# Order of the projections in two attention mixers: queries and keys first, values next, the gate last

## The chip, the cores and the metric

One core of a Trainium2 chip runs the whole program in one launch. The metric is the device time in microseconds, from the first to the last instruction of one execution and what lies around them; several executions are timed and the median counts. Engines are named as in the profile: PE (TensorE matmul), PEld (its weight loads), DVE (VectorE), ACT (ScalarE), POOL (GpSimd), SP (SyncE, whose queue issues the DMAs). Each engine works off its own queue in order; semaphores hold an instruction until its inputs are there.

## The reference

Two layers over 256 tokens of width 1024, all in float32. Each layer is a mixer and then a PEER expert lookup; each of these begins with an RMS norm whose scale and shift come from a conditioning vector (adaLN), and ends in a gated residual.

```python
# layer 0, mixer: h (256 x 1024) -> y
z = h @ w_in                                   # mq mk mv mo mi mf bq bk bv
qk = silu(causal_depthwise_conv(concat(mq, mk), conv_w))
hm = mlstm_chunkwise(q, k, mv, mi + igate_b, mf + fgate_b)     # 4 heads of 128, chunks of 128 tokens
hm = rms_norm(hm, mnorm_g) * sigmoid(mo)       # output gate
qb, kb = rms_norm(bq, qn_g), rms_norm(bk, kn_g)                # 8 heads of 64
hb = softmax(qb kb^T * scale - slope * dist, causal) @ bv      # one block of 256: plain causal attention
y = concat(hm, hb) @ w_out

# layer 1, mixer: differential attention, 8 heads, two q/k parts of 64, values of 128
q, k, v = split(h @ w_in);  q, k = rms_norm(q), rms_norm(k)
o = (softmax(q1 k1^T ...) - lam * softmax(q2 k2^T ...)) @ v
y = (rms_norm(o, onorm_g) * (1 - lam_init)) @ w_out

# both layers, PEER: 8 heads, product keys 2 x 128, top 16, 16384 experts
x = x + g2 * sum(gate * gelu(u[idx] . h2) * v[idx])
```

## The kernel before

**Matmuls.** A float32 product is made of three passes. A weight tile of 128 x 1024 is loaded (`raw`), ACT rounds it to a high part (`hi`, line 155), DVE subtracts that from it (`lo`, line 158), and PE takes high by high, high by low and low by high. There are three buffers each of `hi` and `lo`. A column tile (`mm_col`, lines 181 to 183) gives 128 output columns on the partitions for 256 tokens: 24 matmuls of 256 columns. A row weight (`mm_row`, lines 233 to 235) gives a quarter of the sum for 512 output columns with the tokens on the partitions: 12 matmuls of 512 columns; four row weights make one row product, in two PSUM buffers.

**Order.** The kernel is written as generators. A mixer's main generator yields after each column tile or row weight (a step); at each step `advance` moves every running side generator (`live`: head pairs, the mLSTM, the norm of q and k) on by one piece. From a certain step on (`SIDE_AT`, `SIDE1_AT`) a step also issues one adaLN product: a 512 KB load and one DVE operation of line 248. `take` keeps weights loaded and split two or three steps ahead in the order of `self.feed`. The framework's planner then sets each engine's order by its own estimate of when inputs are ready, with what is traced earlier going first. `tc.issue_after(x)` adds an edge to it: what is traced under it on the engine of `x` is queued behind `x`, without waiting for `x` to end.

**Mixer 0** (`mixer0`). Column tiles: i = 0 the gate inputs of the mLSTM, 1 to 8 its q and k with the convolution (three DVE operations each, line 509), 9 to 12 its output gate `mo`. Row products of four weights each: the mLSTM's values `mv`, the attention's values `bv`, then q and k of heads 0 to 3 and of heads 4 to 7. `ROWS0` says how many row weights follow each column tile: one each after tiles 4 to 7, twelve after tile 8. The mLSTM starts after all 16. A row product of q and k goes to `qk_norm`: squares on ACT, sums on DVE, the power -1/2 on POOL (`qr`, line 258), the product by it on DVE (`zn`, line 374), transposes on PE (line 382), copies to `z` on ACT. Each head pair then runs `moba_pair`: logits (line 398, in the two PSUM buffers `l`), softmax (lines 408 to 412 and 550), transposes (419 to 421), output (563 to 566). At the end of the mLSTM comes `my`, its output by the gate (line 712). The output projection (`residual`) takes the rows of heads 0 to 5 first, then the mLSTM's, then those of the last two heads.

**Mixer 1** (`mixer1`). Row products in the order q and k of heads 0-1, of 2-3, values of heads 0 to 3, q and k of 4-5, of 6-7, values of 4 to 7. `diff_head` runs logits and two softmaxes per head (784, 785 combine them), waits until its values are there, then transposes, output, norm (`on`, line 808, with the power `oss` on POOL) and the high and low parts for the output projection (814, 815). Softmax tiles `sm_p` have 12 buffers in both mixers.

PSUM has eight buffers: tags `h` and `g` two each, and in the mixers `l` and `t` two each.

Of the kernel before, what the change touches and what calls it, by code (L numbers as in the profile page):

```python
# [20 lines left out]
P = 128  # L21
# [21 lines left out]
LATEP = (None, None, (None, 3))  # L43
ROWS0 = {4: 1, 5: 1, 6: 1, 7: 1, 8: 12}
AHEAD = 2
# [29 lines left out]
class Prog:  # L75
# [251 lines left out]
    def alibi(self, pool):  # L327

        nc = self.nc
        di = pool.tile([P, T], I32, tag="sm_p", name="dist_i", bufs=12)  # L330
# [24 lines left out]
    def qk_norm(self, pool, pss, heads):  # L355
# [16 lines left out]
        for ps, r in zip(pss, rs):  # L372
            z = pool.tile([P, 512], F32, tag="zn", name="zn", bufs=QK_ROWS)
            nc.vector.tensor_tensor(out=split(z), in0=split(ps), in1=r.unsqueeze(2).to_broadcast([P, 8, 64]), op=ALU.mult)
            zn.append(z)
        yield
        for i, begin in enumerate(heads):
# [24 lines left out]
    def softmax(self, pool, lg, h, qt, bias):  # L402

        nc = self.nc
        n = P * (qt + 1)
        p = pool.tile([P, T], F32, tag="sm_p", name="sm_p", bufs=12)
        st = pool.tile([P, 4], F32, tag="sm_s", name="sm_s", bufs=24)
# [17 lines left out]

    def residual(self, layer, gate, w_out, act, kds):
        nc = self.nc
        for dt, ps in self.col_tiles([w_out[i] for i in range(KD)], act, ("h", "h", "l"), kds):
# [13 lines left out]
    def mixer0(self):  # L442
        nc, tc = self.nc, self.tc
        with ExitStack() as st:
# [36 lines left out]
            cols = [w_in[c] for c in cols]  # L481
            row_aps = [self.io["ev_v"][n, w4] for n in range(2) for w4 in range(4)]
            row_aps += [self.io["ev_qk"][n, w4] for n in range(2) for w4 in range(4)]
            self.feed, n = [], 0
            for i in range(3, 13):
                self.feed.append(cols[i])
                self.feed += row_aps[n:n + ROWS0.get(i, 0)]
                n += ROWS0.get(i, 0)
            row_steps = [self.project_rows(lambda w4, n=n: self.io["ev_v"][n, w4], h, dst)
                         for n, dst in ((0, mv[:, :, :, :P]), (1, bv))]  # L490

            def pairs(n):
                heads = [lambda zs, hp=2 * n + k: live.append(self.moba_pair(pool, hp, zs, bv[:, :, 0], bias, yhi, ylo))
                         for k in range(2)]
                return self.qk_rows(pool, lambda w4: self.io["ev_qk"][n, w4], h, "gh"[n],
                                    lambda pss: live.append(self.qk_norm(pool, pss, heads)))
            row_steps = chain(*row_steps, pairs(0), pairs(1))
            nrow, started = 0, False
            tag0 = lambda i: "t" if min(ROWS0) < i <= max(ROWS0) else "h" if i < 9 or i > 10 else "g"
            for i, ps in self.col_tiles(cols, h, ("h", "h", "l"), ws=ws, rest=tag0):  # L500
                if i == 0:
# [9 lines left out]
                else:  # L511
                    nc.scalar.copy(mo[:, i - 9, :], ps)
                if i == 6:
                    bias = self.alibi(pool)
# [12 lines left out]
                for _ in range(ROWS0.get(i, 0)):  # L527
                    next(row_steps)
                    nrow += 1
                    self.advance(live)  # L530
                    yield
                if i >= 8 and nrow >= 4 and not started:
                    live.append(self.mlstm(pool, rows, qk, mv, mo, yhi, ylo))
                    started = True
            while live:
                self.advance(live)
            yield from self.residual(0, 16, self.io["ev_out"], (yhi, ylo), (4, 5, 6, 0, 1, 2, 3, 7))

    def moba_pair(self, pool, hp, zs, bv, bias, yhi, ylo):

# [6 lines left out]
        for qt in range(TT):  # L547
            for hh in range(2):
                p, rc, n = self.softmax(pool, lgs[hh], 2 * hp + hh, qt, bias)
                nc.vector.tensor_scalar_mul(p[:, :n], p[:, :n], rc)  # L550
                pr[hh].append(p)
            yield
        pts = []
# [166 lines left out]
    def mixer1(self):  # L720
# [4 lines left out]
        with ExitStack() as st:  # L725
# [7 lines left out]
            with tc.issue_after(self.last_h.ins), tc.issue_after(self.last_t.ins):  # L733
                self.qk_setup(pool, Cols.od_qn, Cols.od_kn)
                og = pool.tile([P, 1], F32, name="og")
                nc.vector.tensor_scalar_mul(og, self.small[:, Cols.onorm:Cols.onorm + 1], 1.0 - LAM_INIT)
                bias = self.alibi(pool)
            v = pool.tile([P, TT, 1024], F32, name="v")
# [16 lines left out]
            self.ready = ws  # L755
            self.feed = od_qk[0][3:] + od_qk[1] + od_v[0] + od_qk[2] + od_qk[3] + od_v[1]
            for i, _ in enumerate(chain(heads(0, "h"), heads(1, "g"), values(0), heads(2, "g"), heads(3, "h"), values(1))):
                if i == 5:
# [11 lines left out]
            while live:  # L770
                self.advance(live)
            yield from self.residual(1, 16, self.io["od_out"], (yhi, ylo), range(KD))

# [472 lines left out]
```

## Time and profile before

| | us |
|---|---|
| median of 3 runs | 1953.21 (1952.89 to 1954.54) |
| the profiled execution | 1958.02 |
| its span, first to last instruction | 1956.2 |
| mean granted PE clock | 0.987 |

The span holds, in this order: loading and the first norm (to 33 us), mixer 0 (to 190), PEER of layer 0 (to 1000), mixer 1 (to 1143) and PEER of layer 1. The granted clock is a share of PE's full 2.4 GHz. A row of a view that ends in `[3.43 <-DVE sm_s L408]` says that the engine was idle for 3.43 us before the instruction and what ended that.

### The profile page before, as it was taken

The page shows a single profiled execution, that of the slowest core. Times are in us where ns is not written, and L with a number is a line of the kernel's source. Part 1 is how long each engine was busy: PE and PEld are TensorE (multiplying, and loading weights), DVE is VectorE, ACT ScalarE, POOL GpSimd, SP SyncE. Part 2 cuts the span into 40 slices and gives each one's busy share as a digit, 9 for nine tenths or more (in the row PEclk, how much of TensorE's full clock was granted, in tenths as well). Part 3 has the DMA queues.
Part 4 walks back from the last instruction along what each step waited for, and adds up shares of the span by engine and source line. Part 5 has one row for each costly group of instructions (what it writes and reads, how often), then busy time and mean ns, then how long its engine had stood idle before and what let it go on. Part 6 is the DMA issues. An engine that isn't in the chain of part 4 may idle for free.

```text
span 1956.2 us, 31712 instructions
## 1 busy us (share of the span) xinstructions
PE 1895.7 (97%) x11733; PEld 1666.4 (85%) x11733; DVE 1524.4 (78%) x3183; ACT 1164.1 (60%) x2249; POOL 40.5 (2%) x37
## 2 busy tenths in 40 slices
PE   4988999999999999999999999999999999999999
PEld 4877999989999788888877799999999988888887
DVE  8886999789998656688568889988899965556655
ACT  4664555688876544444446654568888754444443
POOL 0010000000000000000001200000000000000000
PEclk9999999999999999999989999999999999999999
DMA  8872355555555677898447343554555556669760
GB/s 326 291 255 66 122 171 189 170 164 162 170 159 177 196 216 222 301 366 294 147 150 248 119 146 117 184 183 157 168 164 167 165 172 194 194 199 358 226 197 22
DMA packets 103979, 376.24 MB, mean 192 GB/s; under 512 B 11536, under 2 KB 12944, under 8 KB 103696
## 3 DMA queue, kind: packets, MB, share of 16 engines
q1 hardware_dynamic: 103824, 374.22, 57.7%
q8 instruction: 92, 1.51, 0.3%
q14 instruction: 63, 0.52, 0.1%
HBM read 373.12 MB, written 1.05 MB: 191 GB/s over the span
## 4 chain that ended last, share of the span: by engine, by line
PE 84%; DVE 7%; issue 4%; ACT 2%; DMA 1%; POOL 1%; POOLq 0%; DVEq 0%; ACTq 0%
PE ps_h L976 13%; PE ps_acc L928 12%; PE ps_acc L929 12%; PE ps_acc L927 12%; PE ps_h L181 7%; PE ps_h L183 7%; PE ps_h L182 7%; PE ps_h L980 6%; PE ps_g L1131 3%; DVE lo L158 2%; DVE raw L248 2%; PE ps_acc L999 1%; DMA raw<-in_ev_qk_dram 1%; POOL qr L258 1%; ACT hi L155 1%
## 5 line engine op out<-in xcount | busy, mean ns | idle before, releaser
L155 ACT CAST hi<-raw 128x1024 fp32r<-128x1024 f32 x613 | 645.5, 1054 | 585.2 <-PE ps_acc L928 309.8
L158 DVE TENSOR_TENSOR lo<-raw,hi 128x1024 fp32r<-128x1024 f32 x613 | 747.9, 1221 | 303.1 <-ACT hi L155 296.0
L927 PE MATMUL ps_acc<-hi,act 128*128 128x512 f32 x1024 | 398.2, 390 | 4.4 <-ACT act L908 4.4
L928 PE MATMUL ps_acc<-hi,act 128*128 128x512 f32 x1024 | 400.5, 391 | 0.3 <-DVE act L909 0.2
L929 PE MATMUL ps_acc<-lo,act 128*128 128x512 f32 x1024 | 400.5, 391 | 0.0
L976 PE MATMUL ps_h<-h,hi 128*128 128x512 f32 x1088 | 391.1, 400 | 0.0
L181 PE MATMUL ps_h<-h,hi 128*128 128x256 f32 x1216 | 349.9, 288 | 6.9 <-ACT h L465 3.4
L183 PE MATMUL ps_h<-h,lo 128*128 128x256 f32 x1216 | 345.9, 285 | 0.5 <-DVE lo L158 0.4
L182 PE MATMUL ps_h<-h,hi 128*128 128x256 f32 x1216 | 345.4, 284 | 0.8 <-DVE h L467 0.8
L980 PE MATMUL ps_h<-h,lo 128*128 128x256 f32 x1088 | 281.4, 279 | 0.0
L181 PEld LDWEIGHTS ps_h<-h,hi 128*128 128x128 f32 x1216 | 233.9, 193 | 9.2 <-ACT h L465 4.5
L182 PEld LDWEIGHTS ps_h<-h,hi 128*128 128x128 f32 x1216 | 234.1, 193 | 3.5 <-DVE h L467 1.3
L183 PEld LDWEIGHTS ps_h<-h,lo 128*128 128x128 f32 x1216 | 233.9, 192 | 1.9 <-DVE lo L158 1.2
L976 PEld LDWEIGHTS ps_h<-h,hi 128*128 128x128 f32 x1088 | 201.0, 188 | 35.3
L927 PEld LDWEIGHTS ps_acc<-hi,act 128*128 128x128 f32 x1024 | 192.4, 188 | 44.8 <-ACT act L908 4.8
L928 PEld LDWEIGHTS ps_acc<-hi,act 128*128 128x128 f32 x1024 | 193.1, 189 | 41.2 <-DVE act L909 1.2
L929 PEld LDWEIGHTS ps_acc<-lo,act 128*128 128x128 f32 x1024 | 193.2, 189 | 40.5 <-DVE lo L158 0.7
L980 PEld LDWEIGHTS ps_h<-h,lo 128*128 128x128 f32 x1088 | 205.0, 188 | 8.5 <-DVE lo L158 0.5
L248 DVE CUSTOM_DVE_ANT_0 raw<-raw,crow,small 128x1024 f32<-128x1024 f32 x96 | 122.5, 1279 | 22.0 <-DMA raw<-in_ada_w_dram 21.9
L1108 ACT ACTIVATE oi<-iota,it 128x128 f16<-128x128 f16 x320 | 107.9, 402 | 0.0
L1118 DVE TENSOR_TENSOR og<-oj,gt 128x1024 f16<-128x1024 f16 x128 | 87.6, 684 | 3.5 <-PE ps_g L1131 2.8
L984 ACT COPY hs<-ps_h 128x256 f32<-128x256 f32 x136 | 51.1, 376 | 58.0 <-PE ps_h L976 57.8
(318 smaller groups left out, 2240.8 us busy)
## 6 DMA issues: line engine op xcount, KB each, us to landing
raw<-in_uT_dram SPq DMA_DIRECT2D x256, 512.0 KB, 3.6
raw<-in_v_dram SPq DMA_DIRECT2D x256, 512.0 KB, 4.4
raw<-in_ada_w_dram SPq DMA_DIRECT2D x96, 512.0 KB, 5.2
raw<-in_wq_dram SPq DMA_DIRECT2D x32, 512.0 KB, 4.8
raw<-in_od_qk_dram SPq DMA_DIRECT2D x16, 512.0 KB, 5.2
raw<-in_ev_in_dram SPq DMA_DIRECT2D x13, 512.0 KB, 5.4
raw<-in_ev_v_dram SPq DMA_DIRECT2D x8, 512.0 KB, 4.5
raw<-in_ev_qk_dram SPq DMA_DIRECT2D x8, 512.0 KB, 5.2
```

Of the source, the lines that this page charges most:

```text
L155: nc.scalar.copy(hi, raw)
L158: self.last_lo = nc.vector.tensor_tensor(out=lo, in0=raw, in1=hi.bitcast(F32), op=ALU.subtract)
L181: nc.tensor.matmul(ps, lhsT=whi[:, s], rhs=ahi[:, kd, :], start=kd == kds[0], stop=False)
L182: nc.tensor.matmul(ps, lhsT=whi[:, s], rhs=alo[:, kd, :], start=False, stop=False)
L183: nc.tensor.matmul(ps, lhsT=wlo[:, s], rhs=ahi[:, kd, :], start=False, stop=kd == kds[-1])
L248: nc.vector.tensor_tensor_reduce(w, w, self.crow, 1.0, self.small[:, ab:ab + 1], ALU.mult, ALU.add, m)
L927: nc.tensor.matmul(acc[q], lhsT=xhi, rhs=vhi[:, c], start=m == 0, stop=False)
L928: nc.tensor.matmul(acc[q], lhsT=xlo, rhs=vhi[:, c], start=False, stop=False)
L929: nc.tensor.matmul(acc[q], lhsT=xhi, rhs=vlo[:, c], start=False, stop=m == NEXP - 1)
L976: wide = lambda: nc.tensor.matmul(ps, lhsT=whi[:, s], rhs=both[:, kd].rearrange("p a t -> p (a t)"), start=kd == 0, stop=kd == KD - 1)
L980: nc.tensor.matmul(ps[:, :T], lhsT=wlo[:, s], rhs=both[:, kd, 0], start=False, stop=False)
L1108: nc.scalar.activation(oi[:, k, :], self.iota, AF.Square, scale=-1.0, bias=tabs["i"][:, t0 + k:t0 + k + 1])
```

## The change

Mixer 0 now projects q and k of heads 0 to 3 after column tile 4 and, after tile 8, `mv`, q and k of heads 4 to 7, and `bv`. The mLSTM starts when 8 row weights are through (before: 16). A head pair waits with its transposes until `bv` is projected. The mask of the attention is set up at tile 3 instead of 6. The output projection takes all heads' rows first and the mLSTM's last. Column tiles past the third and the row products change PSUM tags. Mixer 1 projects q and k of all heads, then all values, and has 20 buffers of `sm_p`. In both, each `zn` product is queued behind the low part that was traced last, and the two products of a pair come one step apart.

```diff
-ROWS0 = {4: 1, 5: 1, 6: 1, 7: 1, 8: 12}
+ROWS0 = {4: 4, 8: 12}
...
             z = pool.tile([P, 512], F32, tag="zn", name="zn", bufs=QK_ROWS)
-            nc.vector.tensor_tensor(out=split(z), in0=split(ps), in1=r.unsqueeze(2).to_broadcast([P, 8, 64]), op=ALU.mult)
+            with self.tc.issue_after(self.last_lo.ins):
+                nc.vector.tensor_tensor(out=split(z), in0=split(ps), in1=r.unsqueeze(2).to_broadcast([P, 8, 64]),
+                                        op=ALU.mult)
             zn.append(z)
-        yield
+            yield
...
-        p = pool.tile([P, T], F32, tag="sm_p", name="sm_p", bufs=12)
+        p = pool.tile([P, T], F32, tag="sm_p", name="sm_p", bufs=self.n_p)
...
-            row_aps = [self.io["ev_v"][n, w4] for n in range(2) for w4 in range(4)]
-            row_aps += [self.io["ev_qk"][n, w4] for n in range(2) for w4 in range(4)]
+            row_aps = [self.io[name][n, w4] for n in range(2) for name in ("ev_qk", "ev_v") for w4 in range(4)]
...
-            row_steps = chain(*row_steps, pairs(0), pairs(1))
-            nrow, started = 0, False
-            tag0 = lambda i: "t" if min(ROWS0) < i <= max(ROWS0) else "h" if i < 9 or i > 10 else "g"
-            for i, ps in self.col_tiles(cols, h, ("h", "h", "l"), ws=ws, rest=tag0):
+            row_steps = chain(pairs(0), row_steps[0], pairs(1), row_steps[1])
+            nrow = 0
+            for i, ps in self.col_tiles(cols, h, ("h", "h", "l"), ws=ws):
...
+                    if nrow == 16:
+                        rows["bv"] = True
                     self.advance(live)
                     yield
-                if i >= 8 and nrow >= 4 and not started:
-                    live.append(self.mlstm(pool, rows, qk, mv, mo, yhi, ylo))
-                    started = True
+                    if nrow == 8:
+                        live.append(self.mlstm(pool, rows, qk, mv, mo, yhi, ylo))
...
-            yield from self.residual(0, 16, self.io["ev_out"], (yhi, ylo), (4, 5, 6, 0, 1, 2, 3, 7))
+            yield from self.residual(0, 16, self.io["ev_out"], (yhi, ylo), (4, 5, 6, 7, 0, 1, 2, 3), ("g", "g", "l"))
...
+        while not rows.get("bv"):
+            yield
...
+                self.n_p = 20
...
-            self.feed = od_qk[0][3:] + od_qk[1] + od_v[0] + od_qk[2] + od_qk[3] + od_v[1]
-            for i, _ in enumerate(chain(heads(0, "h"), heads(1, "g"), values(0), heads(2, "g"), heads(3, "h"), values(1))):
+            self.feed = od_qk[0][3:] + od_qk[1] + od_qk[2] + od_qk[3] + od_v[0] + od_v[1]
+            for i, _ in enumerate(chain(*[heads(n, "hg"[n % 2]) for n in range(4)], values(0), values(1))):
```

## Rows read from the trace of the kernel before

**Rows 1.** The page's first part: busy us (share of the span) and instructions.
```profile
PE 1895.7 (97%) x11733; PEld 1666.4 (85%) x11733; DVE 1524.4 (78%) x3183; ACT 1164.1 (60%) x2249; POOL 40.5 (2%) x37
```

**Rows 2.** Busy time by stretch: length, PE, PEld, DVE, ACT, POOL, clock, DMA.
```profile
75.20:168.80 93.60, 81.49 (x463) 67.52 (x461) 77.02 (x207) 51.74 (x121) 10.13 (x5) 0.91 0.62 214
1006.60:1122.30 115.70, 107.15 (x538) 85.51 (x538) 98.79 (x303) 73.70 (x190) 23.45 (x17) 0.94 0.51 173
...
75.20:110.30 35.10, 34.08 (x154) 27.63 (x153) 30.14 (x45) 17.16 (x22) 4.15 (x2) 1.00 0.88 308
```

**Rows 3.** The same view, short stretches of row weights, output tiles, and behind a stall.
```profile
98.00:105.00 7.00, 7.00 (x32) 5.79 (x32) 5.56 (x10) 3.65 (x4) 3.28 (x2) 1.00 1.03 367
174.00:186.00 12.00, 12.00 (x102) 12.00 (x102) 9.82 (x15) 6.37 (x10) 0.00 (x0) 1.00 0.02 3
1046.00:1050.50 4.50, 4.50 (x11) 3.53 (x12) 4.27 (x22) 1.03 (x5) 0.00 (x0) 0.51 1.01 380
```

**Rows 4.** Timeline of PE, logits: start us, length us, instruction, count.
```profile
122.79 2.24 PE L398 MATMUL ps_l<-z 64*128 64x256 f32 x8 [3.43 <-DVE sm_s L408]
...
1036.14 0.92 PE L398 MATMUL ps_l<-z 64*128 64x256 f32 x8
...
1043.97 1.99 PE L398 MATMUL ps_l<-z 64*128 64x256 f32 x8 [3.71 <-DVE sm_s L408]
```

**Rows 5.** Waits of PE, 0 to 200 and 930 to 1200 us: total, times, longest.
```profile
PE ps_l L398 <- DVE sm_s L408: 3.4, 1, 3.4
...
PE ps_l L398 <- DVE sm_s L408: 4.4, 2, 3.7
```

**Rows 6.** Waits of DVE, 42.9 to 168.8 and 1006.6 to 1122.3 us.
```profile
DVE ylo L566 <- ACT yhi L565: 3.1, 3, 1.5
DVE zn L374 <- POOL qr L258: 3.0, 2, 1.5
DVE sm_s L412 <- ACT sm_p L411: 2.0, 3, 1.4
...
DVE mnum L701 <- POOL mr L258: 1.8, 1, 1.8
DVE my L712 <- PE ps_t L709: 1.4, 1, 1.4
...
DVE on L808 <- POOL oss L258: 5.1, 7, 2.2
DVE zn L374 <- POOL qr L258: 3.8, 4, 1.5
```

**Rows 7.** Timeline of DVE around the second pair's products in mixer 1.
```profile
1037.72 0.69 DVE L374 TENSOR_TENSOR zn<-ps_g,qr 128x512 f32<-128x512 f32 x1 [1.17 <-POOL qr L258]
...
1038.40 1.22 DVE L158 TENSOR_TENSOR lo<-raw,hi 128x1024 fp32r<-128x1024 f32 x1
1041.14 0.69 DVE L374 TENSOR_TENSOR zn<-ps_g,qr 128x512 f32<-128x512 f32 x1 [1.53 <-POOL qr L258]
```

**Rows 8.** Groups by line, 33 to 190 us: count, busy us, mean ns, idle before.
```profile
L158 DVE TENSOR_TENSOR lo<-raw,hi 128x1024 fp32r<-128x1024 f32 x38 | 46.2, 1217 | 3.7 <-ACT hi L155 3.3 <-ACT qsq L362 0.3
...
L248 DVE CUSTOM_DVE_ANT_0 raw<-raw,crow,small 128x1024 f32<-128x1024 f32 x28 | 35.6, 1277 | 4.0 <-DMA raw<-in_ada_w_dram 4.0
```

**Rows 9.** Timeline of ACT: the sigmoid of the output gate in mixer 0.
```profile
141.18 1.28 ACT L518 ACT_TABLE_LOAD   x1
142.47 1.06 ACT L518 ACTIVATE mo<-mo 128x1024 f32<-128x1024 f32 x1
```

**Rows 10.** Line 258, the powers (ns, min/median/max), and the timeline beside a pair.
```profile
L258 POOL TENSOR_TENSOR qr<-qv,mhalf x12: 1632/2492/2743, 101.7 to 1091.8; 128x8 f32<-128x8 f32 x12
...
1024.33 4.15 POOL L258 TENSOR_TENSOR qr<-qv,mhalf 128x8 f32<-128x8 f32 x2 [7.11 <-DVE qv L365]
...
1025.52 1.23 DVE L158 TENSOR_TENSOR lo<-raw,hi 128x1024 fp32r<-128x1024 f32 x1
```

**Rows 11.** Busy time by stretch of the instructions on `sm_p` alone: DVE.
```profile
1006.60:1122.30 115.70, 21.81 (x64) 0.94 0.51 173
```

More of the change, by code (lines that the diff above doesn't have):

```diff
@@ L329, in alibi @@
         nc = self.nc
-        di = pool.tile([P, T], I32, tag="sm_p", name="dist_i", bufs=12)
+        di = pool.tile([P, T], I32, tag="sm_p", name="dist_i", bufs=self.n_p)
         nc.gpsimd.iota(di, pattern=[[-1, T]], base=P, channel_multiplier=1)
@@ L424, in transpose_p, with residual @@
         return pt
-    def residual(self, layer, gate, w_out, act, kds):
+    def residual(self, layer, gate, w_out, act, kds, tags):
         nc = self.nc
-        for dt, ps in self.col_tiles([w_out[i] for i in range(KD)], act, ("h", "h", "l"), kds):
+        for dt, ps in self.col_tiles([w_out[i] for i in range(KD)], act, tags, kds):
             g = self.mod[:, layer, gate + dt:gate + dt + 1]
@@ L488, in mixer0 @@
                 n += ROWS0.get(i, 0)
-            row_steps = [self.project_rows(lambda w4, n=n: self.io["ev_v"][n, w4], h, dst)
+            row_steps = [self.project_rows(lambda w4, n=n: self.io["ev_v"][n, w4], h, dst, "g")
                          for n, dst in ((0, mv[:, :, :, :P]), (1, bv))]
             def pairs(n):
-                heads = [lambda zs, hp=2 * n + k: live.append(self.moba_pair(pool, hp, zs, bv[:, :, 0], bias, yhi, ylo))
+                heads = [lambda zs, hp=2 * n + k: live.append(self.moba_pair(pool, hp, zs, bv[:, :, 0], bias, yhi, ylo, rows))
                          for k in range(2)]
@@ L512, in mixer0 @@
                     nc.scalar.copy(mo[:, i - 9, :], ps)
-                if i == 6:
+                if i == 3:
+                    self.n_p = 12
                     bias = self.alibi(pool)
@@ L529, in mixer0, with moba_pair @@
                     nrow += 1
+                    if nrow == 16:
+                        rows["bv"] = True
                     self.advance(live)
                     yield
-                if i >= 8 and nrow >= 4 and not started:
-                    live.append(self.mlstm(pool, rows, qk, mv, mo, yhi, ylo))
-                    started = True
+                    if nrow == 8:
+                        live.append(self.mlstm(pool, rows, qk, mv, mo, yhi, ylo))
             while live:
                 self.advance(live)
-            yield from self.residual(0, 16, self.io["ev_out"], (yhi, ylo), (4, 5, 6, 0, 1, 2, 3, 7))
-    def moba_pair(self, pool, hp, zs, bv, bias, yhi, ylo):
+            yield from self.residual(0, 16, self.io["ev_out"], (yhi, ylo), (4, 5, 6, 7, 0, 1, 2, 3), ("g", "g", "l"))
+    def moba_pair(self, pool, hp, zs, bv, bias, yhi, ylo, rows):
         nc = self.nc
@@ L771, in mixer1 @@
                 self.advance(live)
-            yield from self.residual(1, 16, self.io["od_out"], (yhi, ylo), range(KD))
+            yield from self.residual(1, 16, self.io["od_out"], (yhi, ylo), range(KD), ("h", "h", "l"))
     def diff_head(self, pool, hd, zs, v, vhave, bias, lam, og, yhi, ylo):
```

## The prediction

> **What bounds the kernel now.** I read the page first, for who is busy over the whole span, and then only the two mixer stages, since the change touches nothing else. The reader is to see in the page's row that TensorE (PE) is busy 97% of the span [rows 1]: outside the mixers nothing is left to gain by order. So the question is how much of the mixers' time PE does not need.
>
> Second view, busy time in two stretches [rows 2]. The first goes from 75.2 us (nine column tiles and four row weights are through PE, which the new order also has done by then) to 168.8 (the last low part of the attention output is written). The second goes from 1006.6 (first operation of layer 1's norm) to 1122.3 (the same last low part). VectorE (DVE) is busy 77.0 of 93.6 us and 98.8 of 115.7 us: idle 16.6 and 16.9 us.
>
> PE's need is counted from how many matmuls it starts in a stretch without gaps (one of the count is the pieces cut at the ends): 31 of 512 columns in 7.00 us and 101 of 256 in 12.00 [rows 3], so 0.227 and 0.12 us for one, 2.73 for a row weight (12 of them) and 2.9 for a column tile (24). The first stretch holds 12 row weights, four gate tiles and about half of three output tiles: 32.8 + 11.6 + 4, and some 22 us of small matmuls, counted in the same way (for instance four times 0.92 for the logits [rows 4]): 70 of 93.6 us. The second holds 24 weights, most of three tiles (7) and some 26 of small ones: 99 of 115.7. So each stretch has 17 to 23 us that PE doesn't need, and a floor nearly as near on DVE. Neither engine alone explains the loss; the waits between them do.
>
> Third view, who waited for whom. On PE [rows 5] the largest wait inside each of the two stages is that of a logits matmul for a softmax on DVE, 3.4 us and 3.7. Each costs more than its row. Before the stall eight logits matmuls took 0.92 us, right after it 2.24 and 1.99, and from 1046.0 on only some 10 of 512 columns start in 4.50 us, at a granted clock of 0.51 [rows 3]: PE stood still and came back at 1.2 GHz instead of 2.4. The stall of 3.71 is followed by 1.1 us (logits) and some 2 (ten matmuls where 20 would fit) lost in this way: 6.8 in all; the one of mixer 0 comes to about 6 likewise (3.4 + 1.3 + some 1.4).
>
> On DVE [rows 6] I look for waits that stand in its queue with runnable work behind them. The norm-factor product `zn` waits 3.0 us in mixer 0 and 3.8 in mixer 1 for GpSimd's power; `on` waits 5.1 for the same engine; in mixer 0's end `ylo`, `sm_s`, `mnum`, `my` wait 3.1 + 2.0 + 1.8 + 1.4 = 8.3. The order of time shows what a `zn` wait holds up [rows 7]: product (1.17 late), then a weight's low part, then the second product (1.53 late), and only behind that the first softmax of layer 1, for which PE's second logits wait until 1043.97.
>
> **The change part by part.** All sums are against the profiled execution: span 1956.2, 1.8 around it, 1958.0 in all, which is 4.8 over the median of the runs, 1953.2. I take the gain off the median.
>
> *Products behind a later low part.* Each of the 12 pieces (4 + 8) of `zn` now follows the low part of a weight that is used two or three weights later, and the second one is traced a step after the first. The rows show a low part directly behind a product (1038.40 behind 1037.72), so the pin does change DVE's order. A low part takes 1.22 us and the adaLN product that often stands next to it 1.28 [rows 8], about the 1.17 to 1.53 that DVE stood still: the wait is filled, -3.0 and -3.8 of DVE time. What is queued behind `zn`: transposes on PE, z on ScalarE, logits, softmax; and the PSUM pair, which the heads after next need. Those start four weights after the product's own rows end (11 us), the product follows some two weights after, so I price this at nothing; bounds 0 to 3 us (one weight late, once).
>
> *Mixer 0, q and k of the first four heads before the values.* Nothing is added or removed: 37 weight loads, 16 of them row weights, 24 adaLN loads in between from the same step on, all on SP in the new order with the ring of 8. The logits of heads 0 to 3 move from 113 to about 78 us, under row projections; the mLSTM starts after 8 row steps instead of 16, some 22 us sooner. So in the end stretch fewer chains are left, and the 8.3 us of DVE waits there shrink. They don't vanish: the gate is last, and after its fourth tile come copy 0.4, table load 1.28, sigmoid 1.06 [rows 9], the product `my` 1.1, the high part 0.6, the low part 0.7, and 1.8 more for the second half: 7 us. Cover for it is heads' output rows first in the output projection: three tiles by four rows by three matmuls by 0.12 = 4.3 us, so 2.7 are exposed. I take half of 8.3 as gained, 4.2 (bounds 0 and 8.3), and 0.8 for the PE slow time beyond DVE's gain. Sum for mixer 0: 3.0 + 4.2 + 0.8 = 8. Bounds: 0, and DVE's 16.6.
>
> *Gate transposes of the mLSTM.* They take a third buffer of the ring that the first pair now holds, so they wait for its product; their column copy is needed first at the mLSTM's start, 20 us later. Nothing. The new PSUM names in the output projection: nothing, the buffers are drained by then.
>
> *Mixer 1, all heads before the values.* Again no operation more. The second four heads' logits come three weights (8 us) sooner, heads 0 and 1 one step later; the first four heads' outputs wait for the values, eight weights later than before. Gained: the two `zn` waits ahead of the first softmax, and with them the 6.8 us on PE. On DVE: 3.8, and of the 5.1 of `on` the piece that stood behind a `qr` on GpSimd's queue, 2.2, since all `qr` now precede all `oss`; the rest is the chain at the end and stays. About 1 more at the end, where the last two heads' softmaxes no longer follow the last row weight. Sum 7. Bounds: 0, and 16.9.
>
> *20 buffers for the softmax tiles.* Eight heads hold two each until the values are there, and those in flight some more. Eight more KB may make early loads of layer 1 wait for other old tiles; they run 25 us ahead of use. Nothing.
>
> Total: 8 + 7 = 15 off 1953.2: 1938.
>
> *A rule weighed.* The rows have GpSimd's power at 1.63 to 2.74 us for one and the same shape [rows 10]. A low part that began inside a pair of powers (1025.52, in 1024.33 to 1028.48) took 1.23, no longer than any other. The Trainium skill (SBUF — State Buffer, section "Who interferes with whom") says that a VectorE instruction with two SBUF inputs and a GpSimd one that reads SBUF exclude each other, and that the second "fully blocks". By that rule the low part put in the product's place would wait just as long. The trace shows GpSimd's time vary, and no block of DVE.
>
> **The rivals.**
> 1. *Forecast*, the waits named above go: 1938, own range 1930 to 1946; chance 0.48.
> 2. *Most of the floor is reached*: with more runnable work at every time DVE's idle of 33.5 us falls to a fifth: -27, 1926. For it: the waits are short and of many kinds, which is what a wider choice cures. Against: the chains at the start and end of both stages stay, where DVE has little else to do. 0.15.
> 3. *DVE is the bound and gives it back*: the work goes earlier into a stretch where DVE has little room (12 row weights with an adaLN product each), other waits replace those gone: -4, 1949. For it: DVE 30.1 of 35.1 us busy from 75.2 to 110.3 [rows 2]. 0.2, half of it inside the bound of no change.
> 4. *Slower: DVE overrun in mixer 1's q and k stage.* Place: 1035 to 1080. For four weights DVE must do four low parts 4.9, four adaLN products 5.1, two heads' norm 2.8 (two products of 0.69, two reduces taken as long) and softmax 2 x 2.7 (21.81 over eight heads [rows 11]) plus about 1 of small ones: 19. PE needs 10.9 + 1.8 + 1.2 = 13.9. Without value weights between, nothing lets DVE catch up, low parts come late, and PE stalls. Today one such stall costs 6.8; three of them, one for each pair after the first, make 13.6 more than today, against 8 from mixer 0: +6, 1959. Decides from about two stalls of that length. Against: adaLN products needn't come early. 0.11.
> 5. *The product's wait moves onto the low part* (the mutual exclusion): of the 15 the 6.8 of `zn` are lost, 1945. The row at 1025.52 speaks against it. 0.06.
>
> **How the numbers follow.** A measurement of this kernel can't tell 0.2%, 4 us, from no change: faster is under 1949.3, slower over 1957.1. Faster: 0.47 + 0.15 + 0.10 + 0.06 = 0.78; same 0.01 + 0.10 = 0.11; slower 0.11. The range 1923 to 1953 holds the forecast, most of rival 2, all of 3 and 5; outside are rival 4 and the far part of 2.
>
> **What would show it.** Right: `zn` with no idle of DVE before it; the logits waits of 3.4 and 3.7 gone from PE; mixer 0's last `ylo` near 161 and mixer 1's stretch some 7 us shorter; the stages of the expert mixers unchanged in length. Wrong: PE waiting for `lo` in mixer 1's row stage with the clock granted below 1.0 there (rival 4); DVE's idle in both stretches as large as now (rival 3); a low part near 2.5 us beside a power (rival 5); a stall of more than 5 us between the sigmoid and the output projection.

## The result, and the profile after

The changed kernel takes 1934.37 us (median of 3 runs, 1933.43 to 1937.32) where the kernel before took 1953.21: ratio 0.990, 95% interval 0.9886 to 0.9913. Forecast was 1938, in a range of 1923 to 1953.

The profiled execution took 1934.37 as well (span 1932.6), against 1958.02 before. To see where the 23.6 us went I cut both executions at the start of the matmuls that spread a stage's norm factors (line 302). They stand at each mixer's end and at the start of the second mixer. Rows of the kernel after, the first and last start at the end of each row:

```profile
L302 PE MATMUL ps_g<-ident,nr x4: 275/275/376, 175.7 to 176.1; 128*128 128x128 f32 x4
...
L302 PE MATMUL ps_g<-ident,nr x4: 421/421/580, 989.7 to 990.5; 128*128 128x128 f32 x4
...
L302 PE MATMUL ps_g<-ident,nr x4: 275/275/376, 1120.9 to 1121.4; 128*128 128x128 f32 x4
```

| us | up to mixer 0's end | expert stage 0 | mixer 1 | rest |
|---|---|---|---|---|
| before | 191.4 | 813.9 | 138.9 | 812.0 |
| after | 175.7 | 814.0 | 131.2 | 811.7 |
| difference | -15.7 | +0.1 | -7.7 | -0.3 |

So both mixers pay, the expert stages nothing. Forecast were 8 and 7. (The sum is 23.6 and not the medians' 18.8 because the profiled execution before stood 4.8 over its median.)

Busy time of the two stretches that answer to the first two of [rows 2] (same columns; again from nine column tiles and four row weights done, and from the second norm's first operation, to the last low part of the attention output):

```profile
76.40:152.90 76.50, 72.28 (x453) 60.25 (x453) 72.65 (x205) 51.89 (x126) 6.84 (x3) 1.00 0.76 258
990.90:1100.80 109.90, 104.25 (x523) 83.33 (x523) 98.17 (x303) 74.01 (x190) 22.88 (x17) 0.96 0.53 182
```

The first stretch is 17.1 us shorter. DVE's idle time in it fell from 16.6 us to 76.50 - 72.65 = 3.9, which is 12.7; the other 4.4 is DVE work that now lies outside the stretch, 2.4 of it two adaLN products behind it, beside the output projection. The granted clock rose from 0.91 to 1.00. In the second stretch DVE's idle fell from 16.9 to 11.7 and the clock rose from 0.94 to 0.96.

What waits are left on DVE, 44 to 152.9 us and 990.9 to 1100.8, against [rows 6]: no `zn` in either, `ylo` 3.1 became 0.4, `my` 1.4 became 0.3, and no wait for an adaLN transfer, of which there were 4.0 us [rows 8].

```profile
DVE mnum L705 <- POOL mr L258: 1.5, 1, 1.5
DVE lo L158 <- ACT hi L155: 1.4, 2, 1.0
...
DVE ylo L570 <- ACT yhi L569: 0.4, 1, 0.4
...
DVE my L716 <- PE ps_t L713: 0.3, 1, 0.3
...
DVE on L813 <- POOL oss L258: 4.5, 6, 0.9
...
DVE sm_s L414 <- ACT sm_p L413: 1.8, 4, 0.9
```

On PE, 44 to 200 and 990 to 1120 us, the waits for a softmax of 3.4 and 3.7 [rows 5] are gone; others, smaller, have come at both mixers' ends:

```profile
PE ps_t L421 <- ACT pT L425: 2.9, 2, 1.8
...
PE ps_t L818 <- DVE ylo L820: 2.7, 3, 1.4
```

And the place of [rows 7] in mixer 1's second group: DVE goes from a low part straight to the product, does softmax work and one more low part, and takes the second product, with no idle time in brackets anywhere:

```profile
1038.33 1.22 DVE L158 TENSOR_TENSOR lo<-raw,hi 128x1024 fp32r<-128x1024 f32 x1
1039.47 0.68 DVE L375 TENSOR_TENSOR zn<-ps_h,qr 128x512 f32<-128x512 f32 x1
...
1040.68 1.22 DVE L158 TENSOR_TENSOR lo<-raw,hi 128x1024 fp32r<-128x1024 f32 x1
...
1041.96 0.67 DVE L375 TENSOR_TENSOR zn<-ps_h,qr 128x512 f32<-128x512 f32 x1
```

### The profile page after: what moved, and what is told of

It is laid out like the page before. It is cut to its first block, busy times and chain, and to the rows that moved or that the text cites. A ratio compares the mean times of both kernels' runs of the same rounds, so it can differ in the third digit from the quotient of the medians.

```text
span 1932.6 us, 31700 instructions
## 1 busy us (share of the span) xinstructions
PE 1884.6 (98%) x11733; PEld 1657.8 (86%) x11733; DVE 1522.5 (79%) x3183; ACT 1161.8 (60%) x2247; POOL 40.6 (2%) x37
## 4 chain that ended last, share of the span: by engine, by line
PE 89%; issue 5%; DVE 4%; ACT 1%; DMA 1%; POOL 0%; POOLq 0%; SPq 0%; ACTq 0%; DVEq 0%
PE ps_h L981 13%; PE ps_acc L933 12%; PE ps_acc L934 12%; PE ps_acc L932 12%; PE ps_h L181 7%; PE ps_h L183 7%; PE ps_h L182 7%; PE ps_h L985 7%; PE ps_g L1136 3%; DVE lo L158 1%; PE ps_g L234 1%; PE ps_g L235 1%; PE ps_g L233 1%; PE ps_h L233 1%; PE ps_h L235 1%
## 5 line engine op out<-in xcount | busy, mean ns | idle before, releaser
L181 PE MATMUL ps_h<-h,hi 128*128 128x256 f32 x1264 | 362.9, 287 | 7.0 <-ACT h L467 3.7
L183 PE MATMUL ps_h<-h,lo 128*128 128x256 f32 x1264 | 358.9, 284 | 0.4 <-DVE lo L158 0.4
L182 PE MATMUL ps_h<-h,hi 128*128 128x256 f32 x1264 | 358.3, 283 | 0.8 <-DVE h L469 0.8
L985 PE MATMUL ps_h<-h,lo 128*128 128x256 f32 x1088 | 281.4, 279 | 0.0
L181 PEld LDWEIGHTS ps_h<-h,hi 128*128 128x128 f32 x1264 | 242.4, 192 | 9.4 <-ACT h L467 4.7
L182 PEld LDWEIGHTS ps_h<-h,hi 128*128 128x128 f32 x1264 | 242.7, 192 | 3.6 <-DVE h L469 1.3
L183 PEld LDWEIGHTS ps_h<-h,lo 128*128 128x128 f32 x1264 | 242.4, 192 | 1.8 <-DVE lo L158 1.1
L981 PEld LDWEIGHTS ps_h<-h,hi 128*128 128x128 f32 x1088 | 201.0, 188 | 35.3
L985 PEld LDWEIGHTS ps_h<-h,lo 128*128 128x128 f32 x1088 | 205.0, 188 | 8.5 <-DVE lo L158 0.5
```

The lines of the kernel that those rows point to most:

```text
L181: nc.tensor.matmul(ps, lhsT=whi[:, s], rhs=ahi[:, kd, :], start=kd == kds[0], stop=False)
L182: nc.tensor.matmul(ps, lhsT=whi[:, s], rhs=alo[:, kd, :], start=False, stop=False)
L183: nc.tensor.matmul(ps, lhsT=wlo[:, s], rhs=ahi[:, kd, :], start=False, stop=kd == kds[-1])
L981: wide = lambda: nc.tensor.matmul(ps, lhsT=whi[:, s], rhs=both[:, kd].rearrange("p a t -> p (a t)"), start=kd == 0, stop=kd == KD - 1)
L985: nc.tensor.matmul(ps[:, :T], lhsT=wlo[:, s], rhs=both[:, kd, 0], start=False, stop=False)
```

## The experiments

There were twelve runs. Their times spread by several us from execution to execution of one kernel (last section), so the four stage lengths of each profiled execution, cut as above, are read beside the whole time.

| kernel | median us | ratio to before, 95% interval | mixer 0's end | expert 0 | mixer 1 | rest |
|---|---|---|---|---|---|---|
| e1 pin only | 1945.44 | 0.9935 to 0.9964 | 186.5 | 811.3 | 134.2 | 812.2 |
| e2 order only | 1939.71 | 0.9914 to 0.9940 | 175.4 | 812.2 | 138.0 | 811.6 |
| e3 mixer 0 and pin | 1935.77 | 0.9899 to 0.9928 | 175.4 | 811.5 | 133.4 | 812.2 |
| e4 mixer 1 and pin | 1943.49 | 0.9926 to 0.9952 | 187.7 | 811.4 | 131.0 | 811.6 |
| e5 the changed kernel again | 1934.53 | 0.9878 to 0.9908 | 176.3 | 814.0 | 130.9 | 811.7 |
| e6 late mLSTM | 1937.39 | 0.9907 to 0.9934 | 181.7 | 811.4 | 129.5 | 811.6 |
| e7 old output order | 1930.76 | 0.9870 to 0.9901 | 174.3 | 811.7 | 132.3 | 810.0 |
| e8 one step | 1930.55 | 0.9865 to 0.9895 | 173.7 | 815.3 | 132.8 | 811.1 |
| e9 step apart in mixer 1 | 1931.05 | 0.9854 to 0.9887 | 173.7 | 815.0 | 131.6 | 811.6 |
| e10 gate before values | 1929.57 | 0.9852 to 0.9882 | 174.6 | 811.8 | 131.1 | 811.7 |
| e11 values between | 1932.88 | 0.9872 to 0.9911 | 172.6 | 812.2 | 136.8 | 810.1 |
| e12 early mLSTM alone | 1945.48 | 0.9931 to 0.9963 | 185.2 | 811.7 | 135.1 | 811.2 |

The kernel before ran beside them at 1954.95 (e1 to e4), 1953.89 (e5 to e8), 1955.13 (e9 to e11) and 1955.36 (e12).

What a stage length can tell is seen where several kernels have a mixer in common. One and the same mixer 0 ended at 175.7, 176.3 and 175.4 (after, e5, e3), at 186.5 and 187.7 (e1, e4), at 173.7, 173.7 and 172.6 (e8, e9, e11): differences up to 1.2 are noise. The new mixer 1 took 129.5 to 132.3 in seven kernels (after, e4 to e7, e9, e10). The granted clock in its first 10 us was 0.93 in the shortest (e6) and 0.58 in the longest (e7); in the five between, at 0.64 to 0.69, it took 130.9 to 131.6. "Order" stands in what follows for all that e2 keeps of the change: the order of the weights, the mLSTM's start, the wait for `bv`, the mask, the output projection, the PSUM names and the softmax buffers. The mLSTM's start (e6, e12) and the output projection (e7) were tried apart, the mask and the buffers were not.

**e1: the pin alone**, in the old order.

```diff
-            nc.vector.tensor_tensor(out=split(z), in0=split(ps), ...)
+            with self.tc.issue_after(self.last_lo.ins):
+                nc.vector.tensor_tensor(out=split(z), in0=split(ps), ...)
             zn.append(z)
-        yield
+            yield
```

> The kernel before with the norm-factor products alone queued behind the low part traced last, a step apart (both mixers), orders as before. Theory A (the terms of the prediction): DVE's waits for the power go, 3.0 us in mixer 0 and 3.8 in mixer 1, and nothing else: 1946 against 1953. Theory B (the pin only helps where there is other work to fill the gap, which the new order brings): 1951 to 1954. Theory C (the pin is most of the change): 1938 to 1941.

Measured 1945.44, 9.5 off: Theory A's waits, at some 2.7 more than its 6.8. Mixer 0 ends 4.9 earlier (191.4 to 186.5; 3.7 by e4's 187.7), mixer 1 takes 4.7 less (138.9 to 134.2).

**e2: the orders alone**, the changed kernel with the old `zn` lines.

```diff
-            with self.tc.issue_after(self.last_lo.ins):
-                nc.vector.tensor_tensor(out=split(z), in0=split(ps), ...)
+            nc.vector.tensor_tensor(out=split(z), in0=split(ps), ...)
             zn.append(z)
-            yield
+        yield
```

> The changed kernel with the products neither pinned nor a step apart; both new orders and the buffers stay. Theory A: the 6.8 us of waits come back, 1941. Theory B (pin and order work together): more than 8 us come back, 1943 or later, with zn waiting for the power in DVE's queue again. Theory C': the order alone makes the gain, 1934 to 1936.

Measured 1939.71, 15.2 off where e5 has 19.4: nearest to Theory A, with 4.2 lost instead of 6.8. Mixer 0 ends where the changed kernel's does (175.4), without the pin. Mixer 1 keeps nearly its old length, 138.0, and its trace says why: product waits on DVE and the long logits wait on PE are still there (DVE 988 to 1108, PE 988 to 1125 us).

```profile
DVE zn L374 <- POOL qr L258: 3.6, 3, 1.5
...
PE ps_l L398 <- DVE sm_s L408: 3.8, 1, 3.8
```

The first two rows below are DVE's, the others PE's. The logits of 1017.85 were through at 1018.8, and their softmax started at 1023.50, directly behind the second product:

```profile
1022.89 0.69 DVE L374 TENSOR_TENSOR zn<-ps_g,qr 128x512 f32<-128x512 f32 x1 [1.53 <-POOL qr L258]
1023.50 0.28 DVE L408 CUSTOM_DVE_ANT_0 sm_p<-ps_l,alibi 128x128 f32<-128x128 f32 x1
...
1017.85 0.92 PE L398 MATMUL ps_l<-z 64*128 64x256 f32 x8
...
1025.72 1.99 PE L398 MATMUL ps_l<-z 64*128 64x256 f32 x8 [3.75 <-DVE sm_s L408]
```

So the pin, not the order, removes that stall. Of engines' queues the Trainium skill (PSUM — Partial Sum Buffer, section "Engine vs sequencer instructions") says that those of ScalarE, VectorE and GpSimd are strict FIFO. The trace agrees: the softmax that PE wants is ready to run, and starts behind the waiting product.

**e3: mixer 0's order and the pin**, mixer 1 in the old order with 12 buffers.

```diff
-                self.n_p = 20
+                self.n_p = 12
-            self.feed = od_qk[0][3:] + od_qk[1] + od_qk[2] + od_qk[3] + od_v[0] + od_v[1]
+            self.feed = od_qk[0][3:] + od_qk[1] + od_v[0] + od_qk[2] + od_qk[3] + od_v[1]
...
```

> The changed kernel with mixer 1 in its old order (values between the heads, 12 softmax buffers); mixer 0 new, products pinned in both. Theory A: mixer 1 keeps the 3.8 of its products and loses the rest of its 7.7: 1938. Rival: all of mixer 1's gain is its order, 1942. Rival: all of it is the pin, 1934.

**e4: mixer 1's order and the pin**, mixer 0 in the old order (the same lines the other way, in the kernel before).

> The kernel before with mixer 1 new and the products pinned in both mixers; mixer 0 in its old order. Theory A: of mixer 0's 15.7 only the 3.0 of its products stay: 1934.4 + 12.7 = 1947. Rival: mixer 0's gain is all order, 1950. Rival: the pin is most of it, 1938.

Measured 1935.77 and 1943.49, which lies in both between Theory A and the rival that gives all to the pin. By whole times mixer 1's order is worth between 0.2 (19.2 off in e3, 19.4 in e5) and 2.0 (9.5 in e1, 11.5 in e4), too little to tell; by the stage 2.2 to 2.5 (133.4 to 131.2 and 130.9) and 3.2 (134.2 to 131.0, both at a clock of 0.69 in the first 10 us; e3 had 0.83 there). Without the pin it is worth 0.9 at most (138.9 to 138.0), which is within the noise.

**e5: the changed kernel again**, for comparison with e6 to e8.

> The changed kernel once more, so that the three kernels beside it have it on the same chip. Every theory: 1934 to 1936, that is 19 to 20 us under the kernel before; mixer 0's last low part of the attention output near 152.5, the first tile norm of layer 1's mixer near 989, no idle of VectorE before a norm-factor product.

Measured 1934.53: as expected.

**e6: the mLSTM after all 16 row steps.**

```diff
-                    if nrow == 8:
+                    if nrow == 16:
                         live.append(self.mlstm(pool, rows, qk, mv, mo, yhi, ylo))
```

> The changed kernel, but the mLSTM starts after all 16 row steps of mixer 0, as before, instead of after 8. Theory A (new order's 11 us in mixer 0 come from its two long chains, the mLSTM and the heads, no longer both ending behind the last row weight): about half of the 11 goes back, +5 against the changed kernel, 1940, and mnum, ds or my come back as waits of VectorE or TensorE in the gate stage. Rival (putting q and k first is all of it, the mLSTM has slack until the gate's sigmoid anyway): within 1.5 us of the changed kernel.

Mixer 0 ends 5.4 later than in e5 (181.7): Theory A. DVE's waits for `mnum` are 3.6 again (1.9 in the kernel after), and PE waits 3.0 for the mLSTM's high part. Of the whole time 2.9 came back as loss; the expert stage was 2.6 shorter in this execution.

**e12: the early mLSTM alone**, in the old order with the pin. It ran last and belongs beside e6.

```diff
+                if i >= 8 and nrow >= 4 and not started:
+                    live.append(self.mlstm(pool, rows, qk, mv, mo, yhi, ylo))
+                    started = True
                 for _ in range(ROWS0.get(i, 0)):
                     next(row_steps)
...
-                if i >= 8 and nrow >= 4 and not started:
-                    live.append(self.mlstm(pool, rows, qk, mv, mo, yhi, ylo))
-                    started = True
```

> The kernel before with the pin and the step apart, in the old order of weights, and one more thing: the mLSTM starts as soon as its own values and convolutions are there (before the 12 row weights behind the last convolution tile, instead of after them). Pin alone ended mixer 0 at 186.5 and took 1945.4 in all. Theory A (the early start of the mLSTM is worth its 5 us by itself, whatever stands first): mixer 0 ends near 181, 1940. Theory B (only both together empty the end: in the old order q and k come last, so the heads' ends still stand behind the gate and the mLSTM's early work now delays the last weights' low parts): within 1.5 us of pin alone, 186 and 1945. Theory C (the mLSTM's work before the heads' makes the heads later): 188 or more, 1947.

Mixer 0 ended at 185.2, the whole at 1945.48: Theory B. The four kernels show the reason in the rows that write the attention output's low parts. The line with `ps_t` is the heads, that with `my` the mLSTM; the last start of each counts. e1, old order, late mLSTM, both chains end together:

```profile
L568 DVE TENSOR_TENSOR ylo<-ps_t,yhi x4: 410/422/424, 144.7 to 163.4; 128x256 fp32r<-128x256 f32 x4
L718 DVE TENSOR_TENSOR ylo<-my,yhi x2: 678/684/691, 159.6 to 161.5; 128x512 fp32r<-128x512 f32 x2
```

e12, old order, early mLSTM: 11 us earlier on one line, nothing on the other, which now ends the stage alone:

```profile
L568 DVE TENSOR_TENSOR ylo<-ps_t,yhi x4: 415/424/425, 147.9 to 163.5; 128x256 fp32r<-128x256 f32 x4
L718 DVE TENSOR_TENSOR ylo<-my,yhi x2: 686/689/692, 145.8 to 150.2; 128x512 fp32r<-128x512 f32 x2
```

e6, new order, late mLSTM: the heads 13 us earlier, now the mLSTM ends alone:

```profile
L570 DVE TENSOR_TENSOR ylo<-ps_t,yhi x4: 417/424/425, 124.7 to 150.2; 128x256 fp32r<-128x256 f32 x4
L720 DVE TENSOR_TENSOR ylo<-my,yhi x2: 681/687/693, 156.6 to 158.3; 128x512 fp32r<-128x512 f32 x2
```

The kernel after, both:

```profile
L570 DVE TENSOR_TENSOR ylo<-ps_t,yhi x4: 415/422/425, 133.8 to 152.5; 128x256 fp32r<-128x256 f32 x4
L720 DVE TENSOR_TENSOR ylo<-my,yhi x2: 684/684/684, 149.0 to 151.4; 128x512 fp32r<-128x512 f32 x2
```

The early start alone is worth 1.3 (186.5 to 185.2), the rest of the order alone 4.8 (to 181.7), both 10.2 to 11.1 (to 176.3, 175.7 and 175.4); counted from e4's 187.7 each is 1.2 more. Both together give 3 to 5 more than the two apart, which is more than the noise of a stage length.

**e7: the old order of the output projection.**

```diff
-            yield from self.residual(0, 16, self.io["ev_out"], (yhi, ylo), (4, 5, 6, 7, 0, 1, 2, 3), ("g", "g", "l"))
+            yield from self.residual(0, 16, self.io["ev_out"], (yhi, ylo), (4, 5, 6, 0, 1, 2, 3, 7), ("h", "h", "l"))
```

> The changed kernel, but mixer 0's output projection takes its input rows in the old order 4, 5, 6, 0, 1, 2, 3, 7 with the old PSUM names. Theory A (the gate's rows 0 to 3 are written last, at 149 to 152, behind sigmoid and product, so the three tiles' first matmuls have only rows 4 to 6 as cover instead of 4 to 7): one row less cover, 3 tiles x 3 matmuls x 0.12 = 1.1 us, so +1 against the changed kernel, 1936. Rival (the last head pair's row 7 comes as late as the gate, so either order waits): 0 to -1.

Mixer 0 ends 1.1 to 2.0 earlier than in the three kernels that have it otherwise alike (e3, after, e5). That is the rival's sign, at the edge of the noise. Its reason fits the rows: the last low part is the fourth head pair's row 7 (152.5 above), not the gate's (151.4). That row 7 belongs last is likely and not shown, also because the PSUM names changed with it.

**e8: both products in one step**, still pinned.

```diff
             zn.append(z)
-            yield
+        yield
```

> The changed kernel with the pin, but both norm-factor products of a weight group are traced in one step, as before; only the pin is left of that edit. Theory A (the pin does the work, the step apart only spreads the two products over two low parts): 0 to +1.5 against the changed kernel. Rival (the step apart is what keeps a low part between the two products, without it both stand together and delay a low part that TensorE waits for): +3 or more, with a wait of TensorE for lo. Third possibility (the extra step makes the second heads one step late and so lengthens mixer 0's end): -1 to -2.

Mixer 0 ends 2.6 earlier than in e5 (2.0 than after), the third possibility; mixer 1 takes 1.9 longer (1.2 to 1.9 than in the five kernels of like clock, at 0.66 itself). The rows of the second group in mixer 0, first of the kernel after, then of e8 (products on DVE, then the last two heads' logits on PE):

```profile
113.16 0.68 DVE L375 TENSOR_TENSOR zn<-ps_h,qr 128x512 f32<-128x512 f32 x1
117.35 0.68 DVE L375 TENSOR_TENSOR zn<-ps_h,qr 128x512 f32<-128x512 f32 x1
...
131.06 0.92 PE L400 MATMUL ps_l<-z 64*128 64x256 f32 x8
136.02 0.92 PE L400 MATMUL ps_l<-z 64*128 64x256 f32 x8
```

```profile
112.86 1.28 DVE L375 TENSOR_TENSOR zn<-ps_h,qr 128x512 f32<-128x512 f32 x2
...
126.88 0.92 PE L400 MATMUL ps_l<-z 64*128 64x256 f32 x8
132.11 1.41 PE L400 MATMUL ps_l<-z 64*128 64x256 f32 x4 [0.45 <-DVE sm_s L410]
```

The step apart makes the second product 4 us later and both heads' logits likewise, just where the heads end the stage. In mixer 1 the step does not cost this, and without it `zn` waits 1.1 us for GpSimd again and PE 1.0 for a softmax.

**e9: the step apart in mixer 1 only.**

```diff
             zn.append(z)
-            yield
+            if self.n_p == 20:
+                yield
+        if self.n_p == 12:
+            yield
```

> The changed kernel, but the step between the two norm-factor products stays only in mixer 1; in mixer 0 both stand in one step (pinned in both). Theory (the extra step costs mixer 0 some 2.3 us, because its last head pair ends the stage, and gives mixer 1 some 1.7, because there it puts a low part between the products): mixer 0 ends near 173.7 as with one step in both, mixer 1 takes 131 as in the changed kernel; 1930 to 1932, 2 under the changed kernel. Rival (the differences between the earlier runs are the two instruction orders falling into place by chance): any sum, 1930 to 1936, with mixer 1 at 132 to 133.

173.7 and 131.6: each mixer as its theory said, mixer 1 by 1.2 against e8 at a like clock (0.64 and 0.66 in the first 10 us). Whole time 1931.05, though the expert stage took 815.0 in the profiled execution.

**e10: gate tiles before the heads' values**, on top of e9 (also other PSUM names, and five buffers of `pT` instead of three).

```diff
-ROWS0 = {4: 4, 8: 12}
+ROWS0 = {4: 4, 8: 8, 12: 4}
...
-        while not rows.get("bv"):
+        while hp >= 2 and not rows.get("bv"):
             yield
         pts = []
         for hh in range(2):
             pts.append(self.transpose_p(pool, *pr[hh]))
             yield
+        while not rows.get("bv"):
+            yield
...
+            yield from self.residual(0, 16, self.io["ev_out"], (yhi, ylo), range(KD), ("g", "g", "l"))
```

> The kernel e9, and in mixer 0 the four gate tiles stand before the heads' four value weights instead of behind them, the first two pairs transpose their probabilities before the values are there, and the output projection takes the mLSTM's rows first. Theory (what is left at mixer 0's end is the chain behind the gate, table load 1.28, sigmoid 1.06, product, high and low part, over its cover): this chain falls under the value weights (10.9 us on TensorE), and behind the last value weight stand two pairs' transposes and four pairs' products: 2 to 4 us under e9, mixer 0 ending near 170 to 172. Rival (VectorE is full there, 3.9 us idle in 76, so any order ends when its work is done): within 1 us of e9. Third (the four pairs' ends in one row, about 1.5 us of ScalarE and TensorE each, are longer than the gate's chain): 2 to 3 us over e9.

174.6, so within 1 us of e9: the rival's number, but not its reason. DVE is idle 75.60 - 69.55 = 6.1 us from 76.4 to 152.0. PE is busy 73.7 of the 75.6 us in e10 and 73.8 in e9, but at a clock of 0.98 and 1.00 (rows of e10, then e9):

```profile
76.40:152.00 75.60, 73.72 (x456) 61.78 (x455) 69.55 (x198) 53.60 (x127) 6.74 (x3) 0.98 0.71 238
```

```profile
76.40:152.00 75.60, 73.81 (x463) 61.20 (x461) 72.28 (x204) 52.03 (x126) 6.84 (x3) 1.00 0.77 262
```

The low parts of e10 show what happened. The mLSTM's last one starts 12 us earlier than in e9 (151.5), the heads' last one 2 us later (149.9), so the gate's chain is out of the way, as the theory wanted, and the heads end the stage alone, as the third possibility feared:

```profile
L575 DVE TENSOR_TENSOR ylo<-ps_t,yhi x4: 414/420/425, 145.8 to 151.8; 128x256 fp32r<-128x256 f32 x4
L725 DVE TENSOR_TENSOR ylo<-my,yhi x2: 681/685/689, 134.9 to 139.3; 128x512 fp32r<-128x512 f32 x2
```

**e11: four heads' values between the third and the fourth group**, on top of e9.

```diff
-            self.feed = od_qk[0][3:] + od_qk[1] + od_qk[2] + od_qk[3] + od_v[0] + od_v[1]
+            self.feed = od_qk[0][3:] + od_qk[1] + od_qk[2] + od_v[0] + od_qk[3] + od_v[1]
...
```

> The kernel e9, and in mixer 1 the first four heads' value weights stand between the third and the fourth group of q and k weights. Theory (mixer 1's gain is the pin's; its order is worth 2 to 3 us because GpSimd's powers of the heads' norms no longer stand between those of q and k): mixer 1 takes 1 to 2 us longer than in e9, 132 to 133. Rival (with all values last, eight heads' ends crowd behind them, and spreading them fills VectorE's waits for oss): 1 to 3 us shorter, 128 to 130.

Mixer 1 takes 136.8, 5.2 longer than in e9: the theory's sign, at more than twice its size. PE has new waits in 988 to 1125 us, for a value weight's low part and for a head's scaled output. The theory's reason is not borne out: the last group's powers do come between those of the heads' norms, but DVE waits 4.4 for `oss` and 0.2 for `qr`, where e9 has 4.5 and 0.2. What costs the 5.2 is open.

```profile
PE ps_t L821 <- DVE on L816: 1.7, 2, 1.0
...
PE ps_g L234 <- DVE lo L158: 1.3, 1, 1.3
```

e7 to e10 stand 23.1, 23.3, 24.1 and 25.6 us under the kernel before, against 19.4 for e5. Their intervals overlap e5's, and their mixers together are only 0.6 (e7) to 1.9 (e9) shorter than e5's; that they beat the kernel before is shown, that they beat the changed one is likely for e9 and e10 and not shown.

## Why the prediction was right, and where not

The total came near, 1934 against 1938, and the waits named were the right ones, but part of the nearness is luck. By stages the mixers gained 23.4 where the sum had 15; the terms were read from an execution 4.8 over the median, and taken off the median.

*Products behind a later low part: right, undersized.* No `zn` waits, as forecast, and the logits waits went with them. The term counted DVE's 3.0 and 3.8; e1 measured 4.9 and 4.7. The difference fits what PE lost behind the stall, which the prediction had priced (6.8 in mixer 1) and, but for 0.8 in mixer 0, not added: from 30 to 50 us into mixer 1 the granted clock was 0.91 and then 0.75 before and 1.00 in e1, with 72 matmuls and 104. The wait that it feared behind the pin is real: the extra step, priced together with it at 0 to 3, costs mixer 0 1.7 to 3.7 (173.7 and 172.6 without it, 175.4 to 176.3 with it), and is repaid in mixer 1 by 1.2 to 1.9 (e8).

*Mixer 0's order: the mis-sized term.* "I take half of 8.3 as gained, 4.2 (bounds 0 and 8.3), and 0.8": 5.0, where the runs show 10.2 to 11.1 on top of the pin, and 16.0 without it (e2). Four things were off.

The largest is likely PE's slow time, put at 0.8. From 120 to 170 us the granted clock was 0.83 before, 0.90 in e1 and 1.00 after (in this order):

```profile
120.00:170.00 50.00, 39.55 (x247) 32.82 (x248) 38.69 (x140) 28.02 (x87) 1.64 (x1) 0.83 0.36 126
120.00:170.00 50.00, 42.23 (x281) 34.90 (x280) 38.66 (x144) 31.68 (x93) 1.64 (x1) 0.90 0.34 112
120.00:170.00 50.00, 45.78 (x364) 41.72 (x363) 44.58 (x119) 30.73 (x65) 2.61 (x1) 1.00 0.50 172
```

Taken as lost PE time that is 8.5, 5 and 0 us, an estimate from these rows and an upper one: e5, the changed kernel again, has 0.93 there, 3.5 us in the same count, and ends 0.6 later than the kernel after (it had 11 matmuls more behind it at 120 us). How much of the gain is the clock's and how much the waits' own is not separated.

Then, the 8.3 left out the DVE waits for adaLN transfers, 4.0 [rows 8], which are gone too. What they cost is not shown: with the pin alone they grew, and mixer 0 ended 4.9 earlier all the same (e1, 44 to 170 us):

```profile
DVE raw L248 <- DMA raw<-in_ada_w_dram: 7.8, 7, 2.1
```

Third, the halving rested on a chain behind the gate that would stay; but the heads and the mLSTM had ended together behind it. `ylo`, `sm_s` and `my`, 6.5 together, fell to 2.3 with the pin alone (e1) and to 0.7 with the order, while `mnum` kept 1.5 of 1.8; so the larger part of these waits went with the pin and not with the order to which the sum gave them. And last, the terms were summed as if independent: with the new order pin and step together are worth nothing in mixer 0 (175.4 without both, 175.4 to 176.3 with both) and the pin in one step 1.7 to 2.8 (173.7 and 172.6), though without it `zn` waits 2.8 us there (e2). Pin 4.9 and order 16.0 overlap by some 5.

*The chain behind the gate: named rightly, no longer alone.* Table load and sigmoid stand at 143.63 and 144.92, and the last low part is at 152.5, not near 161. What PE waits for there are ACT's copies `pT`, each of which frees a PSUM buffer for the transposes of a last head. The copy that ends the longer wait stands on ACT directly behind the table load and the sigmoid, so these cost through ACT's queue and not by the path over `my` that was priced (PE, then ACT, the kernel after):

```profile
142.68 0.33 PE L421 MATMUL ps_t<-ident,sm_p 128*128 128x128 f32 x1 [1.07 <-ACT pT L425]
...
146.40 0.33 PE L421 MATMUL ps_t<-ident,sm_p 128*128 128x128 f32 x1 [1.83 <-ACT pT L425]
...
143.63 1.28 ACT L519 ACT_TABLE_LOAD   x1
144.92 1.06 ACT L519 ACTIVATE mo<-mo 128x1024 f32<-128x1024 f32 x1
145.89 0.46 ACT L425 COPY pT<-ps_t 128x384 f32<-128x384 f32 x1
```

The step apart has its share: in e8, where the last heads' logits and transposes come earlier, both waits are gone, and 1.0 for `pT` is left at other matmuls (0.8 in the kernel after). The new order of the output projection, taken as cover for the gate, cost 1.1 to 2.0 (e7), at the edge of the noise: no stall of 5 us.

*Mixer 1: right in sum, wrong in parts.* 7.7 against 7. The pin gives 4.7 of it and the order 2.2 to 3.2, near the 3.2 forecast (2.2 of `on` and 1). But `on` shrank by 0.6 only, 5.1 to 4.5; its longest wait fell from 2.2 to 0.9 (1.5 in e1, 0.9 in e2), so the piece behind a `qr` did go, and others grew. By which wait the order gains the rest is open. The two are no substitutes here: order without pin gives 0.9 at most, and the stall of 3.8 stays.

*Rivals.* The second (most of the floor) came true in mixer 0 alone, where DVE's idle fell to under a quarter; over both stretches 33.5 became 15.6. The third fell. The fourth fell: from 990 to 1120 us PE has no wait for `lo`; its four kinds of waits there are the norm's first operand (1.1) and those of the last heads. The fifth fell by the longest low part of the execution, 1228 ns in 613, beside powers from 1635 to 2745:

```profile
L158 DVE TENSOR_TENSOR lo<-raw,hi x613: 1187/1224/1228, 28.7 to 1918.4; 128x1024 fp32r<-128x1024 f32 x154
...
L258 POOL TENSOR_TENSOR qr<-qv,mhalf x12: 1635/2067/2745, 64.3 to 1052.2; 128x8 f32<-128x8 f32 x12
```

If the two engines exclude each other, as the Trainium skill has it (SBUF — State Buffer, section "Who interferes with whom"), the wait shows here on GpSimd's side only. Nor does every meeting cost it one: a low part that began inside a power (1035.06, in 1034.19 to 1035.83) took 1.23, and that power 1.64, the shortest there is.

## What to carry to other kernels

Where two chains end a stage together, moving either one alone gains little (1.3 and 4.8 here) and both together more than the sum (10.2 to 11.1): find the last start of each chain's last write before pricing a reorder. An instruction that waits in an in-order queue costs its wait and what the next engine loses after the stall; put it behind work that is ready, but only as far as its own consumers have slack, which may differ from stage to stage. And do not take the length of the waits for their price: the pin nearly doubled DVE's waits for transfers in mixer 0 and still gained 4.9, while PE's time at the lower clock, priced at 0.8, came to some 8.5 us before and to none after, an estimate.

## What was not expected of the hardware

One kernel's executions differ by up to 11 us (e11, 1929.87 to 1940.84), and one place of it shows: the first expert stage takes 811.3 to 812.2 us in nine of the fourteen traces and 813.9 to 815.3 in five (before, after, e5, e8, e9), with the same instructions. The two groups part in one stretch of 10 us, 450 us into the stage. PE stands still there for 1.65 us in the kernel after and for 1.55 in e1. Behind that the clock falls to 0.50, 1.2 GHz, for some 3 us in the one, and stays at 1.00 in the other (two rows of after, then two of e1):

```profile
625.70:635.70 10.00, 8.30 (x38) 6.57 (x37) 7.25 (x10) 5.66 (x7) 0.00 (x0) 0.83 0.64 210
...
629.70 1.21 PE L932 MATMUL ps_acc<-hi,act 128*128 128x512 f32 x4 [1.65 <-ACT act L913]
```

```profile
636.50:646.50 10.00, 8.40 (x45) 6.81 (x44) 8.15 (x10) 5.97 (x8) 0.00 (x0) 1.00 0.69 210
...
640.22 1.21 PE L929 MATMUL ps_acc<-hi,act 128*128 128x512 f32 x4 [1.55 <-ACT act L910]
```

In this stretch the five long ones have 0.83 to 0.85 and the nine short ones 1.00. That makes 1.7 us, an estimate from the row, of the 1.7 to 2.7 by which before, after and e5 are longer. The stage's last 10 us differ too (0.82 in after, 0.97 in e1), but e2 and e11 have 0.81 and 0.80 there and take 812.2; e8 and e9, the longest, also have 0.91 in the stage's first 20 us, where the others have 1.00. Why the clock falls behind one gap and not behind the other was not tried; it hides a change of 2 us in the whole time that the stage lengths show.
